# A hybrid convolution and delta-rule layer in two phases: front in three column parts, decay rates computed ahead, diagonal blocks by small operations

## The chip, the cores and the metric

One core of a Trainium2 chip runs the whole layer in one launch. The metric is device time in microseconds, the median of the runs of a kernel. All numbers here are fp32 at the outside; inside, every large product is made of three fp32r matmuls (high times high, low times high, high times low).

## The reference

One layer on x (2048 tokens x 1024), conditioned by a vector c:

```
mod = silu(c) @ w_ada + b_ada            # shift, scale, gate for the mixer and for the FFN
h = rms_norm(x, g) * (1 + scale_m) + shift_m
gate_b, gate_c, h_conv, q, k, v, z, a, bt = split(h @ w_in)      # 3592 columns
ya = group_norm(gate_b * conv3(gate_c * h_conv))
q, k, v = silu(conv4([q, k, v])); q, k normalised per head (4 heads of 128)
beta = sigmoid(bt); g = -exp(a_log) * softplus(a + dt_bias)
# per chunk of tokens: tri = I + strict_lower((k beta) k^T * decay(g)); solve tri for u, w
# then a scan over the chunks with the 128x128 state of each head -> o
yb = rms_norm(o, g_dn) * silu(z)
x = x + gate_m * ([ya, yb] @ w_out)
x = x + gate_f * ((silu(h2 @ W_g) * (h2 @ W_u)) @ w_down)     # h2: x, normalised and modulated
out = rms_norm(x) * (1 + scale_o) + shift_o
```

`a` and `bt` have 4 columns each. "Rates" below are g and beta of one token block, and the decay factors made from g.

## The kernel before

**Stages.** The 2048 tokens are four blocks of 512, numbered 0 to 3. Phase one is the modulation vector, norm and w_in projection of blocks 0 and 1, done together by a seven-product scheme (tiles A11, A12, S1 to S4, A22 of the transposed, modulated x); its results for q, k, v, z, the convolution branch (`ya`) and a/b go to DRAM. Phase two, the mixer, goes through `STAGES` (L410): while the dense strips of the projection of blocks 2 and 3 run on TensorE (14, 14, 12 and 16 strips, `dense_strip` L1680), the delta rule of blocks 0, 1, 2 and 3 is worked in between, one block per stage, and `output(b)` (L1735) closes a stage with the product of [ya, yb] with w_out. Then come the FFN and the final norm, which the change leaves alone.

**The front.** `ada_raw` (L824) loads w_ada columns in two halves of 512 for scale and shift. The first halves are summed by TensorE (`sums_pe` L838, matmuls of one output column, L842), the second halves by VectorE (`sums_dve` L846) and a column sum over partitions (`col_sums` L478, L481). x is transposed (`turned` L858), scaled by ScalarE (`scaled` L855) and split into a high and a low part. The first product of a strip needs A11 (the first four 128-column groups of x), the second needs A12 (the last four).

**The work in between.** Work beside the dense matmuls is written as generators in a list. `dmm` (L317) issues one dense matmul and calls `tick` (L292) after every third; a tick advances each generator whose wait is over. A generator that yields an integer waits so many ticks, one that yields tiles waits until `Clock`, a planner with a cost per instruction (L54), has its tensor engine past the time at which these tiles are ready. In phase two `Clock.pin` (L201) fixes the order of each engine's instructions, and of the DMAs on the SP queue, by the planned times. So waiting is decided when the program is written; on the chip each engine goes through its own fixed order and waits where something in it is late.

**One block of the mixer** (`start_block` L1225). `load_chain` (L1258) loads k, q and z from DRAM. `head_chain` (L1274) loads the block's a and b rows (L1277), transposes them on TensorE (L1281), computes softplus and sigmoid on ScalarE and VectorE (L1285 to L1317), takes cumulative sums of g on TensorE (L1321 to L1323), then builds decay matrices. It goes on, after `after("op")` (the end of the previous block's output), with the Gram matrices k k^T per head on TensorE (M, L1364), and `diagonal_chain` (L1492) picks the 32x32 diagonal blocks out of M: a masked 128x512 product on GpSimd, a VectorE reduction (L1497). The blocks are written to DRAM and read back (L1377 on) so that one partition holds one block. VectorE inverts them in 31 steps (L1393, L1395), the result goes over DRAM again (L1401, L1403) and is spread by masked products into X (L1410). `level_chain` (L1417) joins the 32-blocks to 128 (TensorE, from L1434). `chunk_chain` (L1522) runs the scan over the chunks of 128 tokens, each step waiting for the one before (L1541, L1553, L1561, L1563, then VectorE and back), `out_chain` (L1574) normalises each chunk's output, gates it and transposes it (L1589, L1595). `mix_chain` (L1602) loads the block's `ya` (L1613), normalises it over groups (L1617 to L1631, TensorE at L1624 and L1625) and leaves it as `yah`, `yal` for the output's products. Before the change it starts after `wait("mx")`, that is after the inverse has come back.

**Other pieces that the change touches.** `norm_rows` (L588) normalises and transposes the rows of blocks 2 and 3 during phase one; `back` (L1138) then works off the modulation sums of the later vectors (`mod_gen` L458: eight loads of w_ada rows at L463, one VectorE step for each at L467, the column sum at L481). `project_ab` (L1667) makes the a/b rows of blocks 2 and 3 and stores them (L1675); `build_h` (L1110) reads the normalised rows back, modulates and splits them.

Of the kernel before, what the change touches and what calls it, by code (L numbers as in the profile page):

```python
# [210 lines left out]
def layer_kernel(ctx, tc, x, c, w_ada, b_ada, w_ada_final, b_ada_final, g_norm_mix, g_norm_ffn, g_norm_final,  # L211
# [52 lines left out]
    FIRST_CHAINS = "head_chain", "diagonal_chain", "level_chain", "chunk_chain", "out_chain"  # L264
# [323 lines left out]
    def norm_rows(src, dst):  # L588
        for i in range(CH):
# [4 lines left out]
            for q in range(2):  # L594
                yield 3.0, xt
# [162 lines left out]
    def product(ps, w, a, start):  # L758
        (wh, wl, k0), (ah, al) = w, a
        for k in range(4):  # L760
# [6 lines left out]
    with ExitStack() as actx:  # L767
# [13 lines left out]
        nc.gpsimd.memset(ls.tile([P, 632], F32, name="pad"), 0.0)  # L781
        nc.gpsimd.memset(hal, 0.0)
        kTd, qTd, vd, zd, yad = ([dr.tile([NH, P, BLK], F32, name=f"{n}{b}") for b in range(NB)] for n in ("kT", "qT", "v", "z", "ya"))
        abd = [dr.tile([16, BLK], F32, name=f"ab{b}") for b in range(NB)]
# [39 lines left out]
        def ada_raw(c0, half):  # L824
            for k in range(KD):
                raw = next(slots)
                nc.sync.dma_start(raw, w_ada[k * P:(k + 1) * P, c0 + half * BLK:c0 + (half + 1) * BLK])
                yield k, raw

        def ada_scale(sums, ks):  # L830
            g = Gm[:, ks]
# [3 lines left out]
        def ada_shift(sums, ks):  # L835
            nc.vector.tensor_add(Sm[:, ks], sums, col["b_sm"][:, ks])

        def sums_pe(c0):  # L838
            ps = misc_ps()
            for k, raw in ada_raw(c0, 0):  # L840
                for j in range(4):
                    mm(ps[:, j:j + 1], raw[:, j * P:(j + 1) * P], cs[:, k:k + 1], start=k + j == 0,  # L842
                       stop=k == KD - 1, skip_group_check=True)
            return ps[:, :4]

        def sums_dve(raws):  # L846
            acc = cv_tile([P, BLK])
            for k, raw in raws:
                if k == 0:
                    nc.vector.tensor_scalar_mul(acc, raw, cs[:, 0:1])  # L850
                else:
                    nc.vector.scalar_tensor_tensor(acc, raw, cs[:, k:k + 1], acc, op0=ALU.mult, op1=ALU.add)
            return acc

# [13 lines left out]
        K0, K1 = slice(0, 4), slice(4, KD)  # L868
# [12 lines left out]
        ada_scale(sums_pe(D), K0)  # L881
# [3 lines left out]
        sums = sums_pe(0)  # L885
        raws = {p: [load_strip(PAIRS[p][0])] for p in range(EARLY)}
        late = [list(ada_raw(c0, 1)) for c0 in (D, 0)]
        turns = [turned(0, k, True) for k in range(4)]
        ada_shift(sums, K0)
        kqs = [ra.tile([P, 4, BLK], F32R, name="kq", bufs=2) for _ in range(2)]  # L890
        H["A11"] = kqs
        for k, ps in enumerate(turns):
# [3 lines left out]
        Ws, x0 = {}, {}  # L896
        for p in range(EARLY):
            Ws[p], x0[p] = {}, split_w(raws[p][0], [P, KD, P])
        wab = g0.tile([P, KD, 8], F32, name="wab")
# [87 lines left out]
        def p1(p):  # L987
            a = dense_ps()
            product(a, Ws[p]["B11"], H["A11"], True)
            u = u_tile()  # L990
            nc.scalar.copy(u[:, 4:], a)  # L991
            return a, u

        def p2(p, u):
            b = misc_ps()
            product(b, Ws[p]["B21"], up("A12"), True)
# [39 lines left out]
        opened = []  # L1036
        for p in range(EARLY):
            Ws[p]["B11"], Ws[p]["B21"] = (*x0[p], 0), (*x0[p], 4)
            opened.append(p1(p))
        accs = [sums_dve(r) for r in late]  # L1040
        turns = [turned(0, k) for k in (4, 5, 6)]
        ada_scale(col_sums(accs[0], 4), K1)
        ada_shift(col_sums(accs[1], 4), K1)
        turns.append(turned(0, 7))
        for k, ps in enumerate(turns):
            scaled(raw_d[:, k, :], ps, k + 4)
        del turns, late, accs
        t = ra.tile([P, 2, 4, BLK], F32R, name="r0")
        H["A12"] = [t[:, e] for e in range(2)]
        for k in range(4):  # L1050
            split_one("A12", k, raw_d)
# [11 lines left out]
        def later_sums():  # L1063
# [17 lines left out]
            for n, t in (("S2", raw_a), ("S1", raw_s1), ("S3", raw_c), ("S4", raw_d), ("A22", None)):  # L1081
                if n in ("S4", "A22"):
                    H[n] = [rb.tile([P, 4, BLK], F32R, name=n + i) for i in "hl"]
                for k in range(4):
                    split_k(H[n], k, t[:, k, :] if t is not None else e[k])
# [1261 lines left out]
```

## Time and profile before

| | |
|---|---|
| median of 2 runs | 2570.61 us (2569.17 to 2572.05) |
| the profiled execution: its time | 2568.14 us |
| its span, first to last instruction | 2566.4 us |
| mean granted TensorE clock | 0.967 |
| TensorE busy | 2372.5 us, 92% |
| VectorE busy | 1773.8 us, 69% |
| ScalarE busy | 1097.3 us, 43% |
| GpSimd busy | 620.4 us, 24% |

TensorE is PE in the profile (its weight loads PEld), VectorE DVE, ScalarE ACT, GpSimd POOL, SyncE, whose queue issues nearly all loads and stores, SP. A busy PE is not always one at full speed: a column of the page gives the clock that was granted in each stretch. The two phases lie at 0 to 364 us (phase one) and 364 to about 1250 us (mixer); the rest is FFN and final norm.

### The profile page before, as it was taken

How to read it: one execution, taken by the hardware profiler on the slowest of the kernel's cores; microseconds unless marked ns; L12 is line 12 of the kernel's file. 1: busy time of each engine (PE TensorE's matmuls, PEld its weight loads, DVE VectorE, ACT ScalarE, POOL GpSimd, SP SyncE). 2: the span in 40 equal slices, each digit the busy share in tenths (PEclk: the TensorE clock that was granted, in tenths of full speed). 3: DMA queues.
4: the chain of work that ended last, by engine and by line, in shares of the span. 5: the costliest groups of instructions: out<-in, count | busy, mean ns of one | idle time of the engine just before them, and what ended most of it. 6: DMA issues, size and time to landing. Idle time of an engine off the chain costs nothing. (4 is left out here: it accounts for less than half of the span.)

```text
span 2566.4 us, 31216 instructions
## 1 busy us (share of the span) xinstructions
PE 2372.5 (92%) x11219; PEld 1958.8 (76%) x11219; DVE 1773.8 (69%) x2598; ACT 1097.3 (43%) x1897; POOL 620.4 (24%) x707
## 2 busy tenths in 40 slices
PE   7899977968997986999899999999999999999998
PEld 7677765857876875888777788878888887887786
DVE  3766974963784775577756756687556559788888
ACT  3745545532562552445644333443333333222335
POOL 1222332423514404512100000000000025344437
PEclk9899988969998998999999999999999999999999
DMA  8445564423744551554657633475323337333334
GB/s 293 165 125 172 168 193 153 144 54 91 186 132 123 145 173 42 119 140 147 148 183 231 184 92 114 129 213 152 115 87 110 111 103 270 114 129 119 128 122 154
DMA packets 398309, 370.31 MB, mean 144 GB/s; under 512 B 41653, under 2 KB 320446, under 8 KB 397898
## 3 DMA queue, kind: packets, MB, share of 16 engines
q1 hardware_dynamic: 388538, 351.17, 44.4%
q0 software_dynamic: 4608, 8.39, 2.3%
q10 hardware_dynamic: 5008, 8.76, 0.9%
q8 instruction: 88, 1.44, 0.2%
q14 instruction: 67, 0.55, 0.1%
HBM read 271.64 MB, written 105.01 MB: 147 GB/s over the span
## 5 line engine op out<-in xcount | busy, mean ns | idle before, releaser
L385 ACT CAST whi<-wraw 128x1024 fp32r<-128x1024 f32 x264 | 276.1, 1049 | 379.6 <-PE pd L318 185.0
L387 DVE TENSOR_TENSOR wlo<-wraw,whi 128x1024 fp32r<-128x1024 f32 x264 | 327.1, 1241 | 135.9 <-ACT whi L385 134.3
L318 PE MATMUL pd<-r,whi 128*128 128x512 f32 x1008 | 343.6, 405 | 3.6 <-ACT u L991 2.6
L318 PEld LDWEIGHTS pd<-r,whi 128*128 128x128 f32 x1008 | 192.2, 191 | 44.2 <-ACT u L991 4.0
L318 PE MATMUL pd<-r,wlo 128*128 128x512 f32 x504 | 199.1, 395 | 0.0
L2003 POOL TENSOR_TENSOR ht<-y,ht 128x512 fp32r<-128x512 f32 x1 | 1.4, 1388 | 701.1 <-DMA act<-act 701.1
L2201 DVE TENSOR_TENSOR acc<-acc,pd 128x512 f32<-128x512 f32 x192 | 127.4, 679 | 24.7 <-PE pd L318 24.1
L2081 ACT CAST xh<-ra 128x640 fp32r<-128x640 f32 (+1 forms) x85 | 60.4, 722 | 182.6 <-PE pm L318 134.1
L1943 DVE TENSOR_TENSOR sg<-sg,pd 128x512 f32<-128x512 f32 x44 | 30.2, 686 | 154.1 <-PE pd L318 147.7
L318 PE MATMUL pd<-whi,ym 128*128 128x512 f32 x256 | 89.3, 421 | 26.0 <-ACT ym L1595 26.0
L318 PEld LDWEIGHTS pd<-r,wlo 128*128 128x128 f32 x504 | 96.6, 192 | 16.6
L318 PE MATMUL pd<-A22h,whi 128*128 128x512 f32 x232 | 91.9, 396 | 8.2 <-DVE sg L1943 6.8
L2090 POOL TENSOR_TENSOR xl<-ra,xh 128x640 fp32r<-128x640 f32 (+1 forms) x37 | 61.6, 1665 | 144.1 <-ACT xh L2081 143.3
L2201 DVE TENSOR_TENSOR acc<-acc,pm 128x512 f32<-128x512 f32 x120 | 81.7, 681 | 19.1 <-PE pm L318 18.6
L318 PE MATMUL pm<-S4h,whi 128*128 128x512 f32 x232 | 91.2, 393 | 1.6 <-ACT sg L1937 1.0
L318 PE MATMUL pd<-A22l,whi 128*128 128x512 f32 x232 | 91.7, 395 | 0.0
L318 PE MATMUL pd<-A22h,wlo 128*128 128x512 f32 x232 | 91.2, 393 | 0.0
L318 PE MATMUL pd<-S3l,t3h 128*128 128x512 f32 x232 | 91.2, 393 | 0.0
L318 PE MATMUL pm<-S4l,whi 128*128 128x512 f32 x232 | 90.9, 392 | 0.0
L318 PE MATMUL pm<-S4h,wlo 128*128 128x512 f32 x232 | 90.5, 390 | 0.0
L318 PEld LDWEIGHTS pd<-whi,ym 128*128 128x128 f32 x256 | 51.6, 202 | 40.9 <-ACT ym L1595 29.3
L2130 POOL TENSOR_TENSOR wraw<-wraw 128x512 f32<-128x512 f32 x40 | 69.9, 1769 | 49.1 <-DMA wraw<-in_w_down_dram 42.4
(527 smaller groups left out, 6812.9 us busy)
## 6 DMA issues: line engine op xcount, KB each, us to landing
wraw<-in_w_gate_up_dram SPq DMA_DIRECT2D x88, 512.0 KB
wraw<-in_w_in_dram SPq DMA_DIRECT2D x86, 512.0 KB
ra<-act SPq DMA_DIRECT2D x80, 448.0 KB
act<-S SPq DMA_DIRECT2D x80, 256.0 KB
act<-act SPq DMA_DIRECT2D x68, 256.0 KB
y<-in_w_ada_dram SPq DMA_DIRECT2D x32, 512.0 KB
wraw<-in_w_out_dram SPq DMA_DIRECT2D x32, 512.0 KB
wraw<-in_w_down_dram SPq DMA_DIRECT2D x22, 512.0 KB
```

What stands on the lines that cost most here:

```text
L318: mm(*args, **kw)
L385: nc.scalar.copy(hi, raw)
L387: (lo_engines.popleft() if lo_engines else nc.vector).tensor_sub(lo, raw, hi.bitcast(F32))
L1943: nc.vector.tensor_add(s5[i], s5[i], a[i])
L2003: nc.gpsimd.tensor_sub(hl[1], item0, hl[0].bitcast(F32))
L2081: nc.scalar.copy(hi, raw[:, c0:c1, :])
L2090: eng.tensor_sub(lo, raw, hi.bitcast(F32))
L2130: nc.gpsimd.tensor_mul(r[:, hs], r[:, hs], gate_f[:, hs])
L2201: nc.vector.tensor_add(accs[s, u][:, ns], accs[s, u][:, ns], ps)
```

## The change

Five parts, all in phases one and two.

1. **Front.** The w_ada columns come in three parts (384, 384 and 256 columns) in place of two halves. For part 0 TensorE sums the scale columns and VectorE the shift columns; for parts 1 and 2 VectorE sums the scale and ScalarE with GpSimd the shift. x groups 3 to 7 are transposed early and put aside unscaled. The first products of the early strips are issued in pieces, three groups of x at once and the fourth later, and the second products of the first two strips in two halves.
2. **Rates ahead.** The first half of `head_chain` becomes `rates`, spawned where the a/b product is made, from its PSUM result without the way over DRAM; the result waits in `decay[b]`.
3. **Gram and inverse.** The rest of `head_chain` becomes `decay_chain` and `gram_chain`; the second no longer waits for `after("op")`. M lies in another buffer (`ch`), the small inverse's working tile in `vt` in place of `yal`, and the masked copy of M is made in `mask_chain` after "op". `v_chain` in turn waits for "mx", the end of the inverse; `mix_chain` waits for "op" in place of "mx".
4. **Diagonal blocks.** Four 32-partition VectorE products per head put the diagonal blocks straight into place (after: L1418), for the GpSimd mask and the VectorE reduction. X is cleared by GpSimd and filled by 32-partition copies, even heads on VectorE, odd ones on ScalarE (after: L1471).
5. **Small ones.** `norm_rows` and `back` wait counted ticks (6 and 4) in place of planned times; odd quarters of S3 and A22 have their low part on GpSimd; k, q and z are loaded by one 1 MB DMA each in place of four.

Instructions before and after: PE 10425 to 10390, DVE 2600 to 2701, ACT 1696 to 1798, POOL 712 to 716, SP 934 to 909. Among ACT's are 46 table loads, 29 before.

The diff, cut to its core:

```diff
-        for q in range(2):
-                yield 3.0, xt
+                yield late or (3.0, xt)
...
+        PARTS = range(3), range(3, 6), range(6, KD)
...
+        def sums_on(eng, raws):
+            acc = cv_tile([P, BLK])[:, :raws[0][1].shape[1]]
+            for k, raw in raws:
+                if eng is nc.gpsimd:
+                    nc.scalar.activation(raw if k else acc, raw, AF.Identity, scale=cs[:, k:k + 1])
+                    if k:
+                        eng.tensor_add(acc, acc, raw)
...
-        ada_scale(sums_pe(D), K0)
+        ada_scale(sums_pe(D, PARTS[0]), PARTS[0])
...
-        sums = sums_pe(0)
+        sums = sums_on(nc.vector, list(ada_raw(0, PARTS[0])))
...
+            g, sh = (sums_on(e, late.pop((c0, n))) for e, c0 in ((nc.vector, D), (nc.gpsimd, 0)))
...
+        for p in range(EARLY):
+            a = dense_ps()
+            product(a, Ws[p]["B11"], H["A11"], True, PARTS[0])
+            opened.append([a])
...
+        for p in range(2):
+            banks.append(misc_ps())
+            product(banks[p], Ws[p]["B21"], H["A12"], True, KS[0])
...
+                    (nc.gpsimd if n in ("S3", "A22") and k % 2 else nc.vector).tensor_sub(lo, src, hi.bitcast(F32))
...
+        def rates(b, ps, late=None):
+            abr = cv_tile([P, BLK])[:16, :]
+            nc.vector.tensor_copy(abr, ps[:16, :])
+            yield late or (2.0, abr)
+            ps = misc_ps()
+            for j in range(CH):
+                nc.tensor.transpose(ps[:, j * 16:(j + 1) * 16], abr[:, j * P:(j + 1) * P], ident[:16, :16])
...
+            yield late or (2.0, g, g_hi, g_lo)
...
+            decay[b] = g_hi, g_lo, eg, beta
...
-            t = cv_tile([P, BLK])[:16, :]
-            nc.vector.tensor_copy(t, ps[:16, :])
-            nc.sync.dma_start(abd[b], t)
+            spawn(rates(b, ps, 6), 3)
...
-                yield from norm_rows([...], xTn[b])
+                yield from norm_rows([...], xTn[b], 6)
...
-                yield clock.pe + 4.0
+                yield 4
...
-                    for h in range(NH):
-                        nc.sync.dma_start(t[:, h, :], d[b][h])
+                    nc.sync.dma_start(t, d[b].rearrange("h p t -> p h t"))
...
+            def decay_chain():
+                while b not in decay:
+                    yield POLL
+                g_hi, g_lo, eg, beta = decay[b]
...
+            def gram_chain():
+                yield from wait("k", NH)
...
-                yield from wait("k", NH)
-                yield from after("op")
...
-                    M = ap_.tile([P, CH, P], F32, name="ym", bufs=8)
+                    M = ch_tile([P, CH, P])
                     nc.vector.tensor_mul(M, h4(pkk), Ed[h])
-                    nc.gpsimd.tensor_mul(M, M, bc(bk[:, h], P))
+                    for r in range(NBASE):
+                        rs = slice(r * BASE, (r + 1) * BASE)
+                        nc.vector.tensor_mul(Dg[rs, h], M[rs, :, rs], bk[rs, h].unsqueeze(2).to_broadcast([BASE, CH, BASE]))
...
-                mxq = tile_of([P, 3, BASE, BASE // 2], "yal")
+                mxq = tile_of([P, 3, BASE, BASE // 2], "vt")
...
-                    for e in range(2):
-                        (nc.vector if h > 1 else nc.gpsimd).tensor_mul(
-                            Xv[:, e], xc[:, e, h * CH:(h + 1) * CH].unsqueeze(2).to_broadcast([P, CH, NBASE, HB]), by_base(HB))
+                    for r in range(NBASE):
+                        rs = slice(r * BASE, (r + 1) * BASE)
+                        to = Xs[h][rs, :, rs].rearrange("p j (c e) -> p e j c", e=2)
+                        src = xc[rs, :, h * CH:(h + 1) * CH, :]
+                        for e in range(2):
+                            if h % 2:
+                                nc.scalar.copy(to[:, e], src[:, e])
+                            else:
+                                nc.vector.tensor_copy(to[:, e], src[:, e])
...
-            def diagonal_chain(M, dst):
-                yield from take("lv", 1)
-                md = lv_tile([P, CH, NBASE, BASE])
-                nc.gpsimd.tensor_mul(md, M.rearrange("p j (b c) -> p j b c", c=BASE), by_base(BASE))
-                yield md,
-                nc.vector.tensor_reduce(dst, md.rearrange("p j b c -> p j c b"), op=ALU.add, axis=AX.X)
+            def mask_chain():
+                for h, M in enumerate(Ms):
+                    nc.gpsimd.tensor_mul(M, M, bc(bk[:, h], P))
+                yield from after("op")
...
             def v_chain(hs):
+                yield from wait("mx", 1)
...
             def mix_chain(m, cv=None):
-                yield from wait("mx", 1)
+                yield from after("op")
```

How the engines' orders move, at three places.

On VectorE at the end of phase one stand the sums for the last modulation vector: L467 takes in one loaded row tile `y`, L486 makes the vector of the column sums (before):

```order
L951 SCALAR_TENSOR_TENSOR cv<-u,pcb,cv 128x512
L467 SCALAR_TENSOR_TENSOR y<-y,cs 128x1024 x4
L486 TENSOR_TENSOR Sf<-pm,pca 128x8
L997 TENSOR_TENSOR u<-u,pm 128x512
L387 TENSOR_TENSOR wlo<-wraw,whi 128x1024
L1129 TENSOR_TENSOR r_2952<-y,r_2951 128x1024 x2
```

and after the change:

```order
L467 SCALAR_TENSOR_TENSOR y<-y,cs 128x1024
L387 TENSOR_TENSOR wlo<-wraw,whi 128x1024
L965 SCALAR_TENSOR_TENSOR cv<-u,pcb,cv 128x512 x7
L1015 TENSOR_TENSOR u<-u,pm 128x512
L965 SCALAR_TENSOR_TENSOR cv<-u,pcb,cv 128x512
L486 TENSOR_TENSOR Sf<-pm,pca 128x8
L965 SCALAR_TENSOR_TENSOR cv<-u,pcb,cv 128x512
```

Four sums in a row stood right ahead of the last vector and of the first steps of `build_h` (L1129); now the last sum stands alone, and `build_h` (L1231) follows only 25 rows after L486. On TensorE 107 dense matmuls stand between the last column sum and the first a/b product of block 2; before, the column sum was followed by what was left of the last strip.

On TensorE in stage 0, the transposes of a/b (before: L1281) and the cumulative sums of g (L1321 on) for the next block stand directly behind each other, ahead of the group sums of the convolution branch (L1624) and of the output's first products (`yah`):

```order
L318 MATMUL pd<-r_2951,wlo 128x512
L1281 MATMUL pm<-ck,cv 128x16 x4
L1321 MATMUL pm<-g,ck 128x16
L1322 MATMUL pm<-g,ones_r 128x16
L1323 MATMUL pm<-g,ck 128x16
L1624 MATMUL pm<-lv,gones_r 128x256
...
L318 MATMUL pd<-whi,yah 128x512
L318 MATMUL pd<-wlo,yah 128x512
```

After the change the two products of block 1 (L1145 for L1281, L1184 for L1321) stand in phase one, behind block 1's a/b product, among the dense matmuls of two strips (`r_817`, and `kd`, `vt`, `zs`: halves of the A tiles) and a transpose of `norm_rows` (L598):

```order
L1145 MATMUL pm<-ck,cv 128x16 x4
L318 MATMUL pd<-r_817,whi 128x512
L318 MATMUL pd<-r_817,wlo 128x512
...
L598 MATMUL pm<-ck,y 128x128 x4
...
L318 MATMUL pd<-S3l,t3h 128x512
L318 MATMUL pd<-zs,t3l 128x512
L318 MATMUL pd<-zs,t3h 128x512
L1184 MATMUL pm<-g,ck 128x16
L1185 MATMUL pm<-g,ones_r 128x16
```

From the transposes to the cumulative sums there are 27 dense matmuls there, and none before. Block 0's stand in the same way in the front; those of blocks 2 and 3 in stages 0 and 2, behind `project_ab`.

On TensorE in stage 1, the scan steps of block 1 (before: L1541, L1553, L1561, L1563) stand in the output, with at most a few `ym` products (the output's products with the delta rule's result) between one and the next:

```order
L1541 MATMUL pm<-state,kq 128x128 x4
L1544 MATMUL pm<-state,kq 128x128 x4
L1553 MATMUL pm<-ch,X 128x128 x4
L1561 MATMUL pm<-ch,kd 128x128 x4
L1563 MATMUL pm<-ch,E 128x128 x4
L1589 MATMUL pm<-ck,ch 128x128 x4
L318 MATMUL pd<-whi,ym 128x512
L318 MATMUL pd<-wlo,ym 128x512
```

After the change the same steps (L1600, L1603, L1612, L1620, L1622) stand among the dense strips, ahead of the output:

```order
L1600 MATMUL pm<-state,kq 128x128 x4
L1603 MATMUL pm<-state,kq 128x128 x4
L1683 MATMUL pm<-lv,gones_r 128x256
...
L318 MATMUL pd<-r_3086,whi 128x512
L318 MATMUL pd<-r_3085,wlo 128x512
L318 MATMUL pd<-r_3085,whi 128x512
L1612 MATMUL pm<-ch,X 128x128 x4
...
L598 MATMUL pm<-ck,wraw 128x128 x4
...
L1620 MATMUL pm<-ch,kd 128x128 x4
```

Between L1603 and L1612 there are now 3 dense matmuls, between L1612 and L1620 there are 21. Block 2 reads alike: its steps stood in its output and now stand among the strips. In block 0 the steps stay in the output, as before.

More of the change, by code (lines that the diff above doesn't have):

```diff
@@ L756, in prep_strips, with product @@
         W["T1"], W["T4"] = (*x, 0), (*x, 4)
-    def product(ps, w, a, start):
+    def product(ps, w, a, start, ks=range(4)):
         (wh, wl, k0), (ah, al) = w, a
-        for k in range(4):
+        for k in ks:
             first = dict(start=start and k == 0, skip_group_check=not start)
@@ L989, in p1, with copied, p2 @@
             product(a, Ws[p]["B11"], H["A11"], True)
+            return a, copied(a)
+        def copied(a):
             u = u_tile()
             nc.scalar.copy(u[:, 4:], a)
[L992 to L996, printed above, removed]
+            return u
+        def p2(p, u, b=None):
+            part = b is not None
+            b = b if part else misc_ps()
+            product(b, Ws[p]["B21"], H["A12"], True, KS[1] if part else range(4))
             nc.vector.tensor_add(u[:, 4:], u[:, 4:], b)
```

258 lines of the change are left out of this document (136 added, 122 removed).

## Prediction

> **What bounds the kernel now.** I read the page first: its row of 40 slices for PE and for the clock.
>
> ```profile
> PE   7899977968997986999899999999999999999998
> PEclk9899988969998998999999999999999999999999
> ```
>
> PE is the bound nearly everywhere, and where it isn't the clock falls as well: in slices 6, 7, 9, 13 and 16 (64 us each), around and in the mixer, and near the start. A table of the mixer by stretches, cut where PE goes from full to gappy, gives the size.
>
> ```profile
> 364.00:430.00 66.00, 39.47 (x154) 30.29 (x153) 27.46 (x45) 23.51 (x34) 5.57 (x10) 0.74 0.54 170
> 430.00:510.00 80.00, 77.78 (x397) 65.00 (x395) 66.00 (x138) 48.40 (x111) 37.65 (x42) 1.00 0.46 139
> 510.00:608.00 98.00, 62.92 (x385) 54.61 (x385) 59.38 (x103) 32.50 (x79) 31.16 (x45) 0.75 0.24 70
> 608.00:752.00 144.00, 142.92 (x795) 120.67 (x795) 98.11 (x175) 72.36 (x149) 43.36 (x57) 0.99 0.56 149
> 752.00:821.00 69.00, 50.49 (x274) 42.36 (x273) 41.56 (x64) 23.52 (x59) 30.23 (x42) 0.88 0.35 110
> 821.00:921.00 100.00, 100.00 (x514) 82.76 (x513) 73.59 (x153) 52.13 (x120) 36.55 (x49) 1.00 0.64 169
> 921.00:1030.00 109.00, 75.52 (x462) 64.06 (x461) 67.43 (x99) 40.70 (x89) 31.92 (x47) 0.87 0.25 78
> 1030.00:1250.00 220.00, 216.80 (x1208) 184.34 (x1206) 163.86 (x265) 109.27 (x230) 63.75 (x88) 1.00 0.52 135
> ```
>
> The columns are length, then busy time of PE, PEld, DVE, ACT, POOL, then the granted clock. Time lost is the idle time of PE plus what the low clock takes. The second lies between busy x (1 - clock), if the low clock was spread evenly, and length x (1 - clock), if all of it fell on busy time. For 364 to 430: idle 66.00 - 39.47 = 26.5, clock between 10.3 and 17.2, so 36.8 to 43.7; I take the middle, 40. In the same way 510 to 608 loses 51 to 60, middle 55; 752 to 821 loses 24.6 to 26.8, middle 26; 921 to 1030 loses 43 to 48, middle 45.5. The other four rows lose about 8 together. The last one matters most: stage 3 holds a whole block's Gram matrices, inverse and scan among its 16 strips and PE is idle 3.2 us in 220. What is lost in stages 0 to 2 is not the work of a block but where it stands.
>
> Then the PE waits by releaser, in windows around these stretches:
>
> ```profile
> PE pm L1281 <- DMA cv<-ab: 13.9, 1, 13.9
> PE pm L481 <- DVE y L467: 11.9, 1, 11.9
> PE pm L1321 <- DVE g L1310: 11.5, 1, 11.5
> PE pd L318 <- ACT ym L1595: 12.5, 4, 7.4
> PE pm L1553 <- DVE ch L1547: 7.6, 4, 5.7
> ```
>
> The first two are the 26.5 us of 364 to 430. The third is block 1's rates standing in the way of block 0's products. The last two are the scan in the outputs of blocks 1 and 2, where PE has nothing but what the scan releases.
>
> **The change, part by part.** *The two waits at 364 to 430.* The timeline shows both as late issues.
>
> ```profile
> 376.68 3.60 PE L481 MATMUL pm<-ones_r,y 128*128 128x16 f32 x16 [11.88 <-DVE y L467]
> 411.51 0.44 SPq L1277 DMA_DIRECT2D cv<-ab  x1
> ```
>
> The order now puts the last sums well ahead, with 107 dense matmuls between them and the first a/b product. The spacing of dense matmuls at full clock:
>
> ```profile
> 396.08 0.39 PE L318 MATMUL pd<-A22l,whi 128*128 128x512 f32 x1
> 396.31 0.39 PE L318 MATMUL pd<-A22h,wlo 128*128 128x512 f32 x1
> ```
>
> so 0.23 us each, and 107 are 24 us, more than the 11.9 us. The load of a/b, issued at 411.51 behind k, q and z on SP, is gone. New here is that k comes as one 1 MB piece behind the last of `build_h` and that the Gram product now wants it at once: 0 to 6 us; I take 3. This stretch goes from 40 to 3: **-37**.
>
> *Rates in phase one.* Alone, the chain from the transposes to g takes 6 us:
>
> ```profile
> 416.82 0.57 PE L1281 MATMUL pm<-ck,cv 16*128 16x16 f32 x4 [13.91 <-DMA cv<-ab]
> 417.66 1.28 ACT L1295 ACT_TABLE_LOAD   x1
> 418.95 0.22 ACT L1295 ACTIVATE sp_e<-ab 128x16 f32<-128x16 f32 x1
> 422.63 0.17 DVE L1310 TENSOR_TENSOR g<-sp_p,nexpa 128x16 f32<-128x16 f32 x1
> ```
>
> For blocks 0 and 1 the order leaves 27 dense matmuls, 6.1 us, between the two. That covers the chain alone, but not behind casts of 1 us on ACT and 1.2 us on DVE, which stand in program order there. If it is late, every dense matmul behind the cumulative sums waits. Bounds: 0, and twice the 11.5 us above. Nearer to the first, since one or two casts are what can be ahead at each of the chain's changes of engine: 2 x 4 = **+8**. Blocks 2 and 3 have far more cover.
>
> 17 more table loads at 1.28 us are 22 us on ACT, which has half its time free; they lie beside PE work, and a scan step or two may see one: **+2**. The Trainium skill ("ScalarE: Activation LUTs", What ACT_TABLE_LOAD costs) adds a drain of 1.38 us to each switch; the trace shows the next instruction 1.29 us after the load's start, so none here. By the page the extra work of ACT would be an estimated 45 us, still within its free time, and the sum some 2 us more.
>
> *Block 0.* The wait for g, 11.5 us, goes. But the inverse is now what PE comes to next. From the a/b product to the first level product (L1434 before) the order has 98 us of PE work at full clock. What DVE must do in that time, by the groups of 419 to 525 before, and the group norm's reciprocal from 400 to 600:
>
> ```profile
> L1206 DVE SCALAR_TENSOR_TENSOR cv<-pd,pcb,cv 128x511 f32<-128x511 f32 (+2 forms) x36 | 26.8, 743 | 9.3 <-ACT cv L1204 8.5
> L387 DVE TENSOR_TENSOR wlo<-wraw,whi 128x1024 fp32r<-128x1024 f32 x14 | 19.0, 1357 | 0.0
> L1393 DVE TENSOR_TENSOR lv<-yal 128x126 f32<-128x126 f32 (+22 forms) x31 | 7.9, 256 | 0.8
> L1395 DVE TENSOR_TENSOR yal<-yal,lv 128x126 f32<-128x126 f32 (+22 forms) x31 | 7.9, 256 | 1.1
> L1497 DVE TENSOR_REDUCE Dg<-lv 128x128 f32<-128x512 f32 x4 | 4.3, 1067 | 0.0
> L1628 DVE RECIPROCAL cv<-cv 128x512 f32<-128x512 f32 x4 | 13.4, 3339 | 6.5 <-ACT cv L1627 6.5
> ```
>
> 36 convolution steps (26.8), 15 low parts (20.4), the 31 inverse steps (15.8), and now also the group norms of the convolution branch, which stood behind the inverse and stand before its end: four reciprocals (13.4) and 12 operations of about 0.7 (8.4). The 16 small products for the diagonal blocks have no row; between the 128x16 operations (0.17) and the 128x126 ones (0.26, though over all partitions) or the four reductions that they replace, they cost 2.7 to 4.3: no change. The rest (kd, M, E, norms, edges, one set of rates) is about 17. Sum 103 to 109. The inverse then makes its way over DRAM:
>
> ```profile
> 518.46 0.17 DVE L1395 TENSOR_TENSOR yal<-yal,lv 128x16 f32<-128x16 f32 x1
> 525.92 0.71 DVE L1428 STREAM_TRANSPOSE lv<-X 128x512 f32<-128x512 f32 x1 [2.51 <-POOL X L1410]
> ```
>
> 7.5 us, and the copies into X, 16 on DVE and 16 on ACT at 0.2, take what the masked products took. So the first level starts 112 to 118 us after the a/b product, PE is there after 98: a new wait of 14 to 20, say 17, and 4 for the clock after it. Its scan stays where it was, in the output:
>
> ```profile
> 545.00:560.00 15.00, 13.78 (x131) 12.83 (x130) 12.18 (x11) 8.04 (x16) 1.89 (x2) 0.87 0.13 36
> 560.00:580.00 20.00, 15.53 (x95) 14.01 (x94) 10.03 (x17) 4.32 (x18) 9.91 (x16) 0.76 0.00 1
> 580.00:610.00 30.00, 22.01 (x120) 18.46 (x120) 12.95 (x19) 8.77 (x24) 15.34 (x22) 0.84 0.32 105
> ```
>
> By the same rule these lose 23 to 25; I keep 24. Block 0 goes from 55 to 24 + 21 = 45, and 2 for the handover of k to block 1's Gram product: **-8**.
>
> *Blocks 1 and 2.* With the Gram matrices in the previous output, the first level product stands some 58 us of PE work earlier in block 1's order, and the scan steps stand between 3 to 21 dense matmuls each (0.7 to 4.8 us), as in stage 3, which loses 3 of 220 us. The DVE work up to block 1's first level is, counted in the same way, about as long as PE's (59 against 57 us with the ways over DRAM), so I leave 6 for each block, a short wait with its clock. 26 to 6 and 45.5 to 6: **-20** and **-39**. If a step's cover is gone it costs a wait as in the rows above, 2 to 6 us each.
>
> *The clock.* The row behind the 11.9 us wait:
>
> ```profile
> 376.70:386.00 9.30, 9.30 (x31) 8.06 (x32) 0.53 (x2) 3.84 (x5) 0.00 (x0) 0.54 0.40 116
> ```
>
> 9.3 us at 0.54 cost 4.3 us, the figure used above. The Trainium skill ("TensorE: Matmul & The Clock Gate", Part 1: The HAM clock gate) has full clock return after some 3.4 us of sustained work, which would make it 1.7; the trace shows it later. By the page the clock's share of what is removed, 33 us by the rows, would be an estimated 13, and the time 2478. I go by the rows.
>
> *The front.* PE's one-column sums end at 40.2 and the first product waits for the casts until 46.3; the second product waits for A12:
>
> ```profile
> 36.78 3.41 PE L842 MATMUL pm<-cs,S3l 128*128 128x1 f32 x16
> 46.27 1.22 PE L318 MATMUL pd<-kq,whi 128*128 128x512 f32 x2 [6.08 <-ACT whi L385]
> 67.84 1.52 PE L318 MATMUL pm<-r,whi 128*128 128x512 f32 x2 [2.10 <-ACT r L616]
> ```
>
> Now 24 column sums stand there in place of 64, and the loads ahead of them are three eighths of w_ada's columns in place of a half: first product at 27 to 30. But the fourth x group and A12 wait for parts 1 and 2, whose shift sums go over ACT and POOL one after the other (7 adds of near 0.8 us each): A12 whole at about 52 instead of 67.8. **-16**, between -8, if the loads set the pace, and -24.
>
> Sum: -37 + 8 + 2 - 8 - 20 - 39 - 16 = -110. From the profiled execution's 2568.1 that is **2458**; the runs shown lie 1 to 4 us above it, which I leave out.
>
> **The rivals.** *VectorE becomes the bound of the mixer.* By the table DVE is busy 597 of 886 us in the mixer, and would be 597 of about 782, 76%. Against it: 75% in stage 3 and 82% in 430 to 510 go with hardly any PE idle. For it: block 0's sum above shows it locally. If blocks 1 and 2 meet it as well, half of their 59 us goes, and block 0's wait is 8 to 12 us longer: 2458 + 30 + 12 = 2500.
>
> *The scans are moved but the waits move with them.* PE's order is fixed: a late inverse holds up the dense matmuls behind its first level as well as the scan. If blocks 1 and 2 gain nothing and the front gains nothing either, because the loads set its pace, it is 2458 + 59 + 16 = 2533, no change that can be told: a measurement of this kernel can tell about 2%, 51 us.
>
> *Slower.* The handover of k and q between blocks, on SP:
>
> ```profile
> SPq L1263 <- PE pm L1541: 90.1, 3, 37.8
> ```
>
> Three waits, 30 us each, in which SP holds everything queued behind, the strips' weights too. Today buffered weights and the output cover them. Now the next block's Gram product stands in the output and wants k 7 us of PE work after the last use of the old one. If each of three handovers starves PE for the longest wait seen and a clock recovery, 3 x (37.8 + 4.3) = 126, the time is 2584. It decides from 37 us for each; the weights buffered ahead speak against it.
>
> **How the numbers follow.** The forecast has 0.63, with 2425 to 2490 as its own range (the bounds of the front, the waits in phase one, and block 0). VectorE as the bound 0.22, waits that move 0.11, the SP handover 0.04. Range 2420 to 2515: 2420 is the forecast with every middle at its better end, 2515 takes in the first rival. Faster by over 2% (below 2519) is the first two cases and a little of the third: 0.87. Within 2%: 0.11. Slower: 0.02.
>
> **What would show it.** Right: no PE wait over 4 us between phase one and block 0's inverse; one wait of 10 to 20 us at the first level product of block 0, released by DVE's copies into X or their transpose; PE at 95% or more in the outputs of blocks 1 and 2; the first dense product before 32 us. Wrong: that wait in all blocks with DVE busy throughout (first rival); waits on `ch` or `ym` among the dense strips (second); weights late on SP after each output (third); waits of 5 us or more at the new L1184 in phase one.

## The result, and the profile after

The changed kernel takes 2502.7 us (median of 2 runs, 2499.4 to 2506.0) where the kernel before takes 2570.6: a ratio of 0.9736, 95% interval 0.9676 to 0.9796. Faster, and inside the stated range of 2420 to 2515, but by 68 us and not by 112, and above the forecast's own 2425 to 2490. Timed once more with the experiments, it took 2494.2 us, ratio 0.9709 (0.9677 to 0.9741). The profiled execution has a span of 2497.6 us, 68.8 less than before.

The page's slices of PE and of the clock, after:

```profile
PE   6899999778999898999999999999999999999997
PEclk8899999889999899999999999999999999999999
```

The holes are fewer and shallower, but two are still there, in slices 8 and 9 and in slice 14. The table of stretches, cut again where PE goes from full to gappy:

```profile
365.00:480.00 115.00, 110.60 (x540) 89.40 (x539) 97.89 (x187) 83.71 (x160) 44.56 (x56) 1.00 0.53 159
480.00:595.00 115.00, 84.42 (x553) 73.34 (x552) 71.99 (x175) 37.23 (x138) 50.88 (x74) 0.87 0.36 96
595.00:650.00 55.00, 43.64 (x240) 35.55 (x239) 33.96 (x74) 23.36 (x45) 9.26 (x10) 0.84 0.46 110
650.00:789.00 139.00, 137.15 (x780) 117.53 (x778) 100.49 (x160) 73.95 (x173) 56.74 (x81) 0.99 0.55 160
789.00:880.00 91.00, 78.86 (x428) 63.86 (x427) 61.24 (x135) 51.85 (x87) 11.45 (x17) 0.91 0.47 127
880.00:985.00 105.00, 100.23 (x569) 86.35 (x568) 85.51 (x148) 55.40 (x146) 55.56 (x74) 0.97 0.47 133
985.00:1170.00 185.00, 178.97 (x986) 151.29 (x985) 128.44 (x197) 94.75 (x174) 31.38 (x48) 0.99 0.50 137
```

By the prediction's rule (idle, and the clock between its two bounds, middle taken) these lose 4, 43, 19, 3, 20, 8 and 8 us, 105 in all, where 364 to 1250 lost 174 before. So nearly the whole gain is in the mixer. (Its first stretch began at 364, 24 us ahead of the first mark below; now it begins at that mark.) Where the gain lies, by marks of the program in the two timelines (the first a/b product of block 2, and the last product of each output):

| us from mark to mark | before | after | difference |
|---|---|---|---|
| start to the first a/b product of block 2 | 388.1 | 365.6 | -22.5 |
| to the end of output 0 | 243.2 | 229.1 | -14.1 |
| to the end of output 1 | 202.4 | 194.3 | -8.1 |
| to the end of output 2 | 213.8 | 195.9 | -17.9 |
| to the end of output 3 | 189.2 | 185.1 | -4.1 |
| to the end | 1329.7 | 1327.6 | -2.1 |

The PE waits after, in four windows (the new numbers: L1496 is the first level product, L1335 with `cv` the transposes of v, L1654 the output's operand `ym`, L1686 the square roots of the group norm):

```profile
PE pm L1496 <- DVE lv L1490: 15.0, 1, 15.0
PE pm L1335 <- DMA cv<-v: 2.5, 2, 1.5
...
PE pd L318 <- ACT ym L1654: 9.2, 4, 3.0
PE pm L1335 <- DMA cv<-v: 9.0, 4, 3.1
...
PE pm L1335 <- DMA cv<-v: 6.5, 2, 4.5
PE pm L1504 <- ACT cv L1686: 3.1, 1, 3.1
...
PE pm L1335 <- DMA cv<-v: 3.4, 1, 3.4
```

The waits for the last sums, for a/b from DRAM and for g in the mixer are gone. The one that was forecast in their place, for block 0's inverse, is there: 15.0 us, forecast 17. Not forecast are the waits for v, 21.4 us in four blocks, and in block 1 they come in a row with the clock low behind them (0.84 in the row from 595). The SP queue in that place, as block 1's inverse goes out (`dx`), and the transposes of v on PE:

```profile
607.61 1.11 SPq L1457 DMA_DIRECT2D dx<-vt  x2
...
613.34 2.37 SPq L1574 DMA_DIRECT2D cv<-v  x2
...
619.27 2.29 SPq L1574 DMA_DIRECT2D cv<-v  x1
...
622.75 1.29 SPq L1574 DMA_DIRECT2D cv<-v  x1
```

```profile
618.29 0.66 PE L1335 MATMUL pm<-ck,cv 128*128 128x128 f32 x4 [2.67 <-DMA cv<-v]
...
624.14 1.11 PE L1335 MATMUL pm<-ck,cv 128*128 128x128 f32 x4 [3.09 <-DMA cv<-v]
627.92 1.09 PE L1335 MATMUL pm<-ck,cv 128*128 128x128 f32 x4 [2.23 <-DMA cv<-v]
```

In blocks 1 to 3 no load of v is issued before the inverse has gone out: `v_chain` waits for it, since v's tile `vt` is now where the inverse is worked. (In block 0 the planned order has the loads ahead of the inverse's end, at 479.5 to 482.9.) The loads also wait for their own buffers `cv`, until stores of the output have landed; SP's waits from 605 to 626 have

```profile
SPq L1574 <- DMA x<-cv: 5.7, 3, 3.0
```

So they are late for two reasons, and PE's fixed order comes to the transposes before they land.

The front's first product, and the first one that needs the second half of A12 (before, all of A12 was first used at 67.84); then GpSimd's shift sums and, beside them, some of VectorE's scale sums:

```profile
29.39 1.22 PE L318 MATMUL pd<-kq,whi 128*128 128x512 f32 x2 [4.37 <-ACT whi L385]
...
61.66 1.22 PE L318 MATMUL pm<-r,whi 128*128 128x512 f32 x3 [2.38 <-ACT r L616]
```

```profile
37.00 3.92 POOL L856 TENSOR_TENSOR cv<-cv,zs 128x384 f32<-128x384 f32 x3
41.00 4.98 POOL L856 TENSOR_TENSOR cv<-cv,S3l 128x384 f32<-128x384 f32 x4
```

```profile
40.08 5.05 DVE L860 SCALAR_TENSOR_TENSOR cv<-vt,cs,cv 128x384 f32<-128x384 f32 x4
```

The first product is where it was forecast, 29.4. The first half of A12 is in use from 51.8; the second half is ready at 61.6 and not at 52. An add of 384 columns takes GpSimd 1.27 us (8.9 over 7), not 0.8, and the adds begin only at 37.0, behind two low parts of weights that the new front also gives to GpSimd (31.8 to 37.0). VectorE's sums of 384 columns take 1.26 us each beside them; before the change, with nothing of the kind on GpSimd, its sums of 512 columns took 0.75 (50.9 to 63.1).

### The profile page after: what moved, and what is told of

Its sections match the earlier page's. It is cut to its first block, busy times and chain, and to the rows that moved or that the text cites. A ratio compares the mean times of both kernels' runs of the same rounds, so it can differ in the third digit from the quotient of the medians.

```text
span 2497.6 us, 31277 instructions
## 1 busy us (share of the span) xinstructions
PE 2344.1 (94%) x11149; PEld 1933.7 (77%) x11149; DVE 1788.2 (72%) x2699; ACT 1140.8 (46%) x1999; POOL 621.3 (25%) x711
## 4 chain that ended last, share of the span: by engine, by line
PE 56%; DVE 10%; DMA 8%; issue 8%; POOL 4%; ACT 4%; SPq 0%; ACTq 0%; DVEq 0%; POOLq 0%
PE pd L318 33%; PE pm L318 16%; DVE acc L2258 1%; DMA cv<-v 1%; DVE wlo L387 1%; DMA x<-cv 1%; DMA y<-in_w_ada_final_dram 1%; DMA wraw<-in_w_gate_up_dram 1%; DVE y L467 1%; PE pm L1335 1%; POOL wraw L2187 1%; PE pm L1504 1%; POOL x L1823 1%; PE pm L1496 1%; PE pm L1600 0%
## 5 line engine op out<-in xcount | busy, mean ns | idle before, releaser
L318 PE MATMUL pd<-r,whi 128*128 128x512 f32 x1008 | 350.0, 410 | 13.2 <-DVE r L1124 8.3
L318 PE MATMUL pd<-whi,ym 128*128 128x512 f32 x256 | 85.3, 406 | 15.8 <-ACT ym L1654 13.9
L2258 DVE TENSOR_TENSOR acc<-acc,pm 128x512 f32<-128x512 f32 x120 | 81.7, 681 | 18.4 <-PE pm L318 17.9
L318 PE MATMUL pd<-S2h,whi 128*128 128x512 f32 x176 | 69.6, 395 | 11.9 <-ACT whi L385 11.1
```

Source lines behind the costliest of these rows:

```text
L318: mm(*args, **kw)
L2258: nc.vector.tensor_add(accs[s, u][:, ns], accs[s, u][:, ns], ps)
```

## The experiments

Twelve runs, in four groups, each group with the kernel before on the same chip. Where not said otherwise an edit is made to the changed kernel. "r_after" is the changed kernel itself, timed in the first group: 2494.2 us.

### r_after: the changed kernel again

> The changed kernel once more, beside the others of this group, as the reference for them: 2495 to 2506 us, ratio to the kernel before 0.971 to 0.976. Every theory expects this.

2494.2 us (2491.2 to 2497.1), ratio 0.9709. Its waits are those above; those for v come to 26 us (2.5 + 12.1 + 11.8). From execution to execution the first mark of the table lies between 362.5 and 367.8 us in the nine profiled executions that share phase one, so differences of under 5 us in it are not read as anything. The two timings of this one kernel, 2502.7 and 2494.2, lie 8.5 us apart; a difference of that size between groups is not read from the times alone.

### r_ticks_only and r_no_ticks: the two waits that count ticks

To the kernel before, for r_ticks_only:

```diff
-                yield 3.0, xt
+                yield 6
...
-                yield clock.pe + 4.0
+                yield 4
```

r_no_ticks is the reverse in the changed kernel.

> The kernel before, with only the counted ticks of the change (norm_rows 6, back 4). Theory (the 11.9 us wait for the last modulation sums goes by this alone, with 4 to 5 us of low clock): 15 to 18 us faster than before, ratio 0.993 to 0.994. Rival (the next thing, the a/b rows of the block over DRAM, is as late as it was, so that the wait of 13.9 us there takes over what is gained): ratio 0.997 to 1.001, with that wait at 20 us or more.

> The changed kernel without the counted ticks (norm_rows and back wait for planned times as before). On VectorE the last four modulation sums then stand in a row again ahead of the last vector. Theory (the ticks alone bring what r_ticks_only showed, whatever the rest): 18 to 29 us slower than r_after, ratio 0.978 to 0.982, with a wait of 10 us or more for the last modulation sums. Rival (with the rest of the change the ticks are worth little, since the inverse of block 0 is late anyway): ratio 0.970 to 0.974.

r_ticks_only: 2538.2 us, ratio 0.9891 (0.9872 to 0.9911), 29 us faster than the kernel before in its group. Two numbers bring more than a third of what the whole change brings. The wait for the last sums is gone, and of the waits behind it none has taken its place:

```profile
PE pm L1321 <- DVE g L1310: 11.6, 1, 11.6
PE pm L1281 <- DMA cv<-ab: 11.4, 1, 11.4
```

The one for a/b is 11.4, before 13.9. The first mark comes at 366.2, 22 us sooner. By the marks stages 0 and 1 are 14 us shorter as well, and stages 2 and 3 7 us longer. The theory is right on the wait, too low on the size. r_no_ticks: 2507.9 us, ratio 0.9772 (0.9753 to 0.9791), 14 us slower than r_after, with the wait back:

```profile
PE pm L481 <- DVE y L467: 11.1, 1, 11.1
```

The first mark is 17 us later. So within the whole change the ticks are worth 14 to 17 us, less than alone and below what was expected; the rival is out.

### r_old_front and r_rates_later: the front, and what stands in it

r_old_front puts halves for parts again, with everything that the diff shows of the front. r_rates_later:

```diff
-        ab_products([(wabs[:, 0:4, :], H["A11"]), (wabs[:, 4:8, :], H["A12"])], 0)
...
             if p == EARLY - 1:
-                ab_products([(wabs[:, 0:4, :], H["S1"]), (wabs2, H["A22"])], 1)
+                ab_products([(wabs[:, 0:4, :], H["A11"]), (wabs[:, 4:8, :], H["A12"])], 0)
+            if p == EARLY:
+                ab_products([(wabs[:, 0:4, :], H["S1"]), (wabs2, H["A22"])], 1)
```

> The changed kernel with the front of before (halves in place of parts, no early transposes, products whole). By the traces the new front has the first product 17 us earlier, but 64 us of products later only 3 us are left, since the tiles of the second block of x then come no sooner. Theory (the rest is given back there): 1 to 6 us slower than the changed kernel, ratio to before 0.971 to 0.974, 2495 to 2503 us. Rival (the forecast's 16 us are there and something else eats them): 2506 to 2513, ratio 0.975 to 0.978.

> The changed kernel with the a/b products of blocks 0 and 1, and with them their rates, one step later in phase one (behind the fourth and the fifth strip). Theory (block 0's rates stand on VectorE and ScalarE among the sums for the S tiles, for which TensorE waits 11 us between 79 and 95): these waits fall by 5 us or more, and the time by 4 to 8 us, ratio 0.967 to 0.970. Rival (the S tiles are late by the load and norm of the second block anyway): within 2 us of the changed kernel, ratio 0.970 to 0.972; the wait for g, 2 us, is the same.

r_old_front: 2501.9 us, ratio 0.9739 (0.9715 to 0.9763), 8 us over r_after; the first mark is at 376.1, 13 us later. The time is in the theory's band, at its edge, and its ground was wrong: by the mark the front is worth 13 us, by the time 8, and the two intervals overlap. Against the kernel before it had looked like 3, probably because phase one also carries the rates now. r_ticks_only, which has the old front and no rates in phase one, reaches the mark at 366.2, r_old_front with them at 376.1: 10 us. (Low parts on GpSimd differ between these two as well; that the 10 us are the rates is argued, not shown.) If so, the front's gain and the cost of the rates nearly cancel.

r_rates_later fell the other way: 2506.6 us, ratio 0.9770 (0.9750 to 0.9790), 12 us slower. In the profiled execution, the slowest of its four (2513.0), the first mark is 19 us later. The waits at the S tiles did not shrink as the theory had it; they come to 8.8 us for 8.3. In r_rates_later:

```profile
PE pd L318 <- DVE r L1124: 5.3, 1, 5.3
...
PE pd L318 <- ACT r L1123: 3.5, 1, 3.5
PE pd L318 <- ACT u L1028: 3.0, 1, 3.0
```

and in r_after:

```profile
PE pd L318 <- DVE r L1124: 8.3, 3, 5.5
...
PE pm L1145 <- ACT nexpa L1155: 2.9, 1, 2.9
```

The wait of 2.9 at the transposes of the rates (L1145) is gone, but others came, of 1 to 3 us, all through the strips that follow: from 100 us to the first mark PE is idle 17.1 us, in r_after 6.0. No single wait explains the 19 us. The theory is out: the rates cost less where they stand than one step later.

### r_gram_op: the Gram matrices after the output again

```diff
             def gram_chain():
                 yield from wait("k", NH)
+                yield from after("op")
```

> The changed kernel, with the Gram matrices of a block again only after the previous block's output. Theory (blocks 1 and 2 gain because the Gram matrices run in the previous output): they lose what they gained, 8 and 18 us, and what the waits for v take now is not added, so 2520 to 2535. Rival (the gain comes from the rates being ready, not from where the Gram matrices stand): within 6 us of 2502.

2517.1 us, ratio 0.9806 (0.9777 to 0.9835), 23 us slower than r_after: the theory, a little under its band. Stage 0 of r_gram_op, and of r_after:

```profile
363.00:579.00 216.00, 183.11 (x992) 151.54 (x990) 147.16 (x289) 109.13 (x233) 80.36 (x109) 0.94 0.45 131
```

```profile
363.00:589.00 226.00, 191.71 (x1085) 160.75 (x1084) 168.92 (x356) 120.13 (x296) 95.25 (x130) 0.95 0.44 128
```

The early Gram matrices lengthen stage 0 by 10 us, 9 of them more PE work (x1085 for x992). By the marks, the three stages behind it are 201, 208 and 196 us in r_gram_op and 195, 198 and 186 in r_after: 7, 10 and 10 us shorter with them. The scan of block 1 stands in the output again, at 710 to 741, where the output's products begin at 704.

### r_mix_mx, r_mix_last and r_wlo_pool: what block 0's inverse waits for

r_mix_mx puts all group norms behind the inverse, r_mix_last the last one of block 0:

```diff
             def mix_chain(m, cv=None):
...
-                yield from after("op")
+                yield from wait("mx", 1)
```

```diff
                 yield from after("op")
+                if b == 0 and m > 2:
+                    yield from wait("mx", 1)
```

r_wlo_pool gives every second low part of stage 0's weights to GpSimd:

```diff
+        lo_engines.extend([nc.vector, nc.gpsimd] * 7)
         B = start_block(0, None)
```

> The changed kernel with the group norms of the convolution branch again behind the inverse, as before (mix_chain waits for mx). Theory (the 15 us wait at the first level product of block 0 is VectorE's queue, in which 22 us of group norms stand ahead of the inverse's end): that wait falls under 6 us although TensorE comes to it 7 us of work earlier; waits of 5 to 12 us come at the group sums or the first output products instead; in all 2495 to 2510. Rival (the inverse is late because of its own length and its way over DRAM): the wait stays at 15 us or grows to 22, and the time grows by 5 to 12 us.

> The changed kernel with one of block 0's four group norms (5.5 us of VectorE) behind the inverse. Theory (VectorE's queue sets the first level product of block 0): the 15 us wait falls to 9 to 11, the time by 3 to 6 us, ratio 0.968 to 0.970. Rival (what r_mix_mx won there it lost behind, so a part does the same): 0.971 to 0.974.

> The changed kernel, with 7 of the low parts of the weights in stage 0 (1.24 us each on VectorE) on GpSimd. Theory (block 0's inverse waits in VectorE's queue): the 15 us wait at the first level product falls by 6 to 9 us, and the time by 6 to 12 us, ratio 0.966 to 0.969. Rival (the low parts are slower on GpSimd, 1.8 to 2.6 us, and hold the strips or slow VectorE, so that as much is lost elsewhere): ratio 0.970 to 0.974.

r_mix_mx: 2501.1 us, ratio 0.9735 (0.9708 to 0.9762), 7 us over r_after and within the theory's band. The wait at the first level product falls to 1.7 us, and others stand in its place:

```profile
PE pm L1335 <- DMA cv<-v: 7.6, 2, 4.5
...
PE pm L1612 <- DVE ch L1606: 5.2, 2, 5.0
PE pd L318 <- ACT yah L1689: 4.9, 1, 4.9
...
PE pm L1496 <- DVE vt L1578: 1.7, 1, 1.7
```

VectorE's last inverse step ends at 468.2 instead of 488.3, 20 us sooner, for 22 us of group norms moved. So the wait is VectorE's queue; that is shown. r_mix_last: 2494.4 us, ratio 0.9723 (0.9706 to 0.9740). The first wait is 9.9, as the theory has it, but the group norm that moved is waited for:

```profile
PE pm L1496 <- DVE lv L1490: 9.9, 1, 9.9
...
PE pm L1685 <- DVE vt L1578: 8.9, 1, 8.9
```

so as to the time the rival is right. r_wlo_pool: 2490.6 us, ratio 0.9710 (0.9690 to 0.9730), the rival too. VectorE lost seven operations of 1.2 us, and the wait fell from 15.3 to 13.8 only. The groups of VectorE from 374 to 490 tell why. In r_after:

```profile
L1451 DVE TENSOR_TENSOR vt<-vt,lv 128x126 f32<-128x126 f32 (+22 forms) x31 | 7.9, 256 | 1.0
...
L1307 DVE TENSOR_TENSOR cv<-cv,halo 128x3 f32<-128x3 f32 x12 | 2.3, 191 | 0.0
L1169 DVE SCALAR_TENSOR_TENSOR sp_p<-sp_p,sp_z 128x16 f32<-128x16 f32 x7 | 1.2, 175 | 0.2
```

and in r_wlo_pool:

```profile
L1451 DVE TENSOR_TENSOR vt<-vt,lv 128x126 f32<-128x126 f32 (+22 forms) x31 | 10.0, 321 | 1.0
...
L1307 DVE TENSOR_TENSOR cv<-cv,halo 128x3 f32<-128x3 f32 x12 | 4.2, 347 | 0.0
L1169 DVE SCALAR_TENSOR_TENSOR sp_p<-sp_p,sp_z 128x16 f32<-128x16 f32 x7 | 3.3, 473 | 0.2
```

The same operations take 2.1, 1.9 and 2.1 us more. In all VectorE is busy 103.2 of these 116 us, and 101.7 in r_after: what was taken off it came back as longer operations on it.

### r_v_slack, r_v_early and r_both: the loads of v

r_v_slack plans TensorE's transposes 4 us later; r_v_early loads v ahead, in one piece, into the tile `zs`, and z after it (blocks 0 to 2); r_both is r_v_early with the edit of r_mix_last.

```diff
-                    yield v, sk
+                    yield 4.0, v, sk
```

```diff
                 if b < 3:
-                    nc.sync.dma_start(B.zs, zd[b].rearrange("h p t -> p h t"))
-                    done["z"] = NH
+                    nc.sync.dma_start(B.zs, vd[b].rearrange("h p t -> p h t"))
+                    done["v"] = NH
...
+                if b < 3 and done["vt"] == NH:
+                    B.zs = tile_of([P, NH, BLK], "zs")
+                    nc.sync.dma_start(B.zs, zd[b].rearrange("h p t -> p h t"))
+                    done["z"] = NH
```

> The changed kernel, with 4 us more planned between the loads of v and their transposes on TensorE. Theory (part of the gain of blocks 1 and 2 is lost because v is now loaded only after the inverse, and TensorE comes to its transposes before the load has landed): the waits for v, 21 us in sum in blocks 0 to 3, fall under 5 us, with the low clock behind them, and the time falls by 12 to 25 us, to 2478 to 2490. Rival (v is only the last of several things that the scan needs): the wait moves to the first scan step or to the level products, and the time stays within 5 us of 2502.

> The changed kernel; for blocks 0 to 2, v is loaded in one piece ahead, into the tile zs, and z is loaded there when v has been used. The order of the level products and the scan steps stays nearly as it is. Theory (TensorE waits 21 to 26 us for late loads of v, and planning it later, as r_v_slack did, only moved the scan behind): the waits for v fall to under 6 us and nothing is moved behind, 12 to 25 us faster than r_after, ratio 0.961 to 0.966. Rival (v is one of several things that are late in blocks 1 and 2, and others, the convolution branch's square roots on ScalarE, the output's products, take over): ratio 0.969 to 0.974.

> v early and one group norm behind the inverse, together. If both theories hold, the sum of both: 15 to 30 us faster than r_after, ratio 0.959 to 0.965. If neither, 0.970 to 0.974.

r_v_slack: 2506.3 us, ratio 0.9759 (0.9732 to 0.9786), 12 us slower than r_after: the rival's time. The waits for v fall to 6.4 us, but PE's fixed order now has other things too early or too late. Its waits from 600 to 800:

```profile
PE pm L1683 <- ACT lv L1678: 10.2, 2, 6.2
...
PE pm L1335 <- DMA cv<-v: 3.6, 2, 3.0
```

r_v_early: 2483.7 us, ratio 0.9685 (0.9664 to 0.9706). From 600 to 1010 no wait for v is left; what is, is spread:

```profile
PE pd L318 <- DVE cv L1832: 6.8, 3, 4.3
PE pm L1145 <- DVE vt L1584: 5.9, 1, 5.9
PE pm L1693 <- ACT lv L1688: 3.9, 1, 3.9
```

Against r_after, stages 1 and 2 are 7 and 12 us shorter (188 for 195, 186 for 198) in the profiled executions, for 20 us of waits for v there. The runs agree: in the eight executions with v's loads and the Gram matrices as in the changed kernel, stage 1 takes 193 to 196 us and stage 2 192 to 198; in r_v_early and r_both it is 187 to 188 and 186 to 190. So the late loads cost about what they seemed to in those stages. In the medians 10 us are left, between the theory's band and the rival's: the first mark came 4 us later, stage 3 is 3 us longer and the rest 5, and why is not tested. Nor does the run part the two reasons for the late loads, for its loads wait for neither the inverse nor a buffer `cv`. It is the fastest of all kernels here, faster than the kernel before by 3.2% and, by medians of different groups, than the changed kernel by 0.4%; the intervals of the two overlap. r_both: 2490.5 us, ratio 0.9702 (0.9687 to 0.9718): 7 us over r_v_early; by its bands neither theory held. Moving the group norm takes away more than it gives, as in r_mix_last.

## Why the prediction was right, and where it was wrong

**The two waits at 364 to 430, -37.** Right. Both are gone, nothing over 2.5 us stands there, and the stretch from 365 to 480 loses 4 us. That the first of them goes by the ticks alone is shown by r_ticks_only and r_no_ticks. Of the other small changes in parts 4 and 5 none was run by itself.

**Front -16, rates in phase one +8.** The net was -8 and is between -5 and 0: the first mark gained 22.5 us, of which the ticks are 17 to 22. The terms: the front 8 to 13 (r_old_front), inside its bounds, the rates about 10 (argued; the waits at the rates themselves are 2.9 and 2.0 us). What was mis-sized in the front is the time until A12 is whole, 61.6 for 52: the adds on GpSimd, 1.27 us for "near 0.8", make 3.3 us of it, and the low parts that stand ahead of them on GpSimd, for which the sum had nothing, 5.2. That these two add up to the delay is argued, not shown.

**Block 0, -8 and a new wait of 17.** Right: 15.0 us, and VectorE needs 113 us from the a/b copy to the last inverse step (375.3 to 488.3 in r_after). Its operations there add up to 108 us, for 103 to 109 in the sum; as some overlap, it is busy 101 of the 113. The end of stage 0 loses 43 us for 45. r_mix_mx shows that the wait is VectorE's queue, and r_mix_last that a part of it can't simply be moved.

**Blocks 1 and 2, -20 and -39.** This is the step that failed: "I leave 6 for each block, a short wait with its clock". The table after has 19 + 3 for block 1 and 20 + 8 for block 2, 50 in place of 12, and that is most of the 44 us by which the forecast was too low. By the marks the two stages gained 26 us of the 59. The Gram matrices did move the scan among the strips (r_gram_op: 23 us). But the sum counted the chain through VectorE only. The change list said that `v_chain` waits for "mx", and nothing was set down for it: v's load, four times 256 KB, then comes behind the inverse, between the inverse's result and the scan. r_v_early shows it, with 19 us in the two stages; it doesn't show how much of that is the inverse and how much the buffers `cv` that the loads wait for. The rest, smaller waits for ScalarE's square roots, the output's buffers and rates, is seen and not tested.

**The rivals.** The time is that of the first, 2500, but its mechanism isn't what happened, so that the two agree, and that the range took the result in, is luck: VectorE bounds block 0, as the forecast itself had it, and in stages 1 and 2 it is busy 69 and 75% (134.45 of 194 us, 146.75 of 196: two rows each of the table of stretches), while PE waits for a DMA. "The waits move with the scans" is nearer for half of its size. The handover on SP did not show: SP's longest wait for the old k or q grew from 37.8 to 43.2 us, and yet the only PE wait for weights in the mixer is one of 0.9 us. Of the signs, PE at 95% in the outputs came true for block 1 (96%, 740 to 789) and not for block 2 (92%, 929 to 985).

## What to carry to other kernels

When a tile moves to another buffer, write down who else uses that buffer, and price the wait that each of them gets, its loads too: that clause of the change had no number. When an order is fixed ahead, try to issue a late transfer earlier before you plan its reader later: here the first took the waits away in two stages, and the second moved them to others that share the order. And try the small constants of a large change by themselves: two of them alone brought 29 of this one's 68 us.

## What the runs showed of the hardware

A small VectorE operation with two operands in SBUF can last until the GpSimd operation beside it has ended. In r_wlo_pool, GpSimd and VectorE at 427:

```profile
427.02 2.40 POOL L387 TENSOR_TENSOR wlo<-wraw,whi 128x1024 fp32r<-128x1024 f32 x1
```

```profile
425.94 3.51 DVE L1169 SCALAR_TENSOR_TENSOR sp_p<-sp_p,sp_z 128x16 f32<-128x16 f32 x7
429.49 0.17 DVE L1170 SCALAR_TENSOR_TENSOR sp_p<-sp_p,sp_s 128x16 f32<-128x16 f32 x1
```

Seven operations that take 1.2 us in r_after take 3.3 here. The last of them, begun 0.2 us after GpSimd's, takes 2.25 us, and the next begins as GpSimd's has ended, at 429.4. The Trainium skill ("GPSIMD Engine Reference", Key points) says that GpSimd shares its SBUF interfaces with VectorE and that instructions with two SBUF inputs contend; the trace agrees, and the price here is the rest of the GpSimd operation, up to 2.3 us for one of 0.17. VectorE's sums in the front, 1.26 us beside GpSimd's adds of the same width, look like the same on larger operations; that is not tested. VectorE's convolution steps, which read one operand from PSUM, keep their 0.75 us beside a GpSimd product of two tiles (r_after, 421.6 to 424.1). GpSimd also takes twice VectorE's time for the same low part, 2.42 against 1.21 us.
